# Hybrid attention trunk on one core: the low part of k laid on all 128 rows, and weight staging in the q/k/v slots

## The chip, the core and the metric

The kernel runs on one core of a Trainium2 chip. The metric is the device time of one execution in microseconds, the median over several runs. A profiled execution gives in addition the span of the program and the time of every instruction on TensorE (PE; its weight loads are listed apart, as PEld), VectorE (DVE), ScalarE (ACT), GpSimd (POOL) and on SyncE's queue (SP), which issues the DMAs.

## The reference, cut to what matters

Two residual layers over 1024 positions of width 1024, each followed by a gated MLP with a short convolution. The first layer splits one projection between differential attention (4 heads, causal) and a pooling mixer, joins both and projects out. The second is sliding-window attention with 16 query heads in 4 groups of 4, window 128. What matters for the change are the scores of both attentions, a product of q and k over 64 channels of a head:

```
# first layer: h heads, m = 2 maps, d = 64 channels
s = jnp.einsum('bqhmd,bkhmd->bhmqk', qi, kf) * scale + bias
# second layer: 128 queries against their own and the previous 128 keys
s = jnp.einsum('bqhgd,bkhd->bhgqk', qi, kb) * scale + bias
```

and the projections by the weights `ab_w_in`, `ab_w_out`, `c_w_in`, `c_w_out`, `w_up` and `w_down`, which the kernel loads in slabs of 128x1024.

## The kernel before

Every fp32 operand is split into a high part, rounded to the fast matmul type, and a low part, the remainder. A product is three matmuls, high*high, high*low and low*high (`mm3`, L96 to L102). A weight slab is loaded by `load_split` (L127): a DMA on SP's queue brings it as fp32 into a staging tile, ACT writes the high part (L109), POOL the low part (L110), both into tiles of the pool tag `ws`. The staging tile is free once POOL has read it.

All large tiles have 4 KB on each of 128 partitions and come from rings by tag, of a fixed number of slots (`BUFS`, L76): `x` 8, `xg` 16, `g` 9, `t` 5, `wr` 2, `ws` 8. `wr` is the staging of raw weights, and of the four slabs of the pooling mixer's result that come back from DRAM (L661). `g` holds the tiles of q, k and v in the attentions, the split result of the pooling mixer and, in the MLP, the gated activations. A tile may be written when the tile that had its slot before is read for the last time; within a tag the slots are handed out in the order in which the program asks for them.

The stages follow each other: the pooling mixer's inputs and the mixer itself (`a_pool`, `a_mix`), the projections of the first layer, its attention (`a_attend`, four heads of eight query blocks j), its output projection, the MLP, the projections of the second layer, its attention (`c_attend`, four groups of eight blocks), its output projection, and the second MLP. While a head or a group runs, other dense work is woven between its blocks by `weave`: the projections of the next heads and groups (L344 is the matmul of `in_tokens` in them), and, in the last two heads and groups, the first part of the output projection (`project_out`, L101 into the banks `psd`). The order of the instructions on each engine is then set by the framework's scheduler from its own estimate of times, so a change in the tiles moves instructions everywhere. Each engine runs its instructions in the order so set.

In a head, `stack_q` builds two tiles of q: in tile m one half of the rows holds the high part of map m's 64 channels, the other half the low part. `stack_k` builds for each m a tile of 128 rows with the high part of k in both halves (L400, L401 on ACT), and one more tile `lo`, in which the rows of half m hold the low part of map m (L402, DVE). A score is two matmuls into one bank (`scores`, L406): L410 contracts 128 rows, (q high; q low) by (k high; k high), and L411 adds q high by k low over the 64 rows of the half m alone. The score then goes to DVE (L481 or L741, which add the table and take the running minimum), to ACT (exp, L485 or L745), through transposes (L505, L763), a second split (L109 on ACT, L110 on DVE, into `hf` tiles), and into the product by v (L516, L101 into `psq`).

Of the kernel before, what the change touches and what calls it, by code (L numbers as in the profile page):

```python
# [13 lines left out]
F32 = mybir.dt.float32  # L14
F32R = mybir.dt.float32r
I32 = mybir.dt.int32
AF = mybir.ActivationFunctionType
# [46 lines left out]
class Trunk:  # L64
# [8 lines left out]
        self.pd = mk("spill", 1, space=bass.MemoryType.DRAM)  # L73
        self.n = 0

    BUFS = {"x": 8, "xg": 16, "g": 9, "t": 5, "wr": 2, "ws": 8}  # L76

    def big(self, tag, dt=F32, shape=(P, 1024)):
        self.n += 1
# [46 lines left out]

    def load_split(self, src, tag="ws", shape=(P, 1024), eng=None):  # L127
        nc = self.nc
        raw = self.big("wr", F32, shape)
        nc.sync.dma_start(raw[:], src)  # L130
        hi = self.big(tag, F32R, shape)
        lo = self.big(tag, F32R, shape)
        with self.urgent():
            self.split(raw[:], hi[:], lo[:], eng or nc.gpsimd)
        return hi, lo
# [252 lines left out]
                    out=dst[other, sl], in0=pt[rows, :], scalar=gain[rows, :], in1=dst[rows, sl].bitcast(F32),  # L388
                    op0=ALU.mult, op1=ALU.subtract)

    def stack_k(self, get, gain, his, lo):
        nc = self.nc
        for h in range(2):
            pt = self.bank()
            for b in range(4):
                nc.tensor.transpose(pt[:, b * P:(b + 1) * P], get(4 * h + b), self.idn[:])
            sl = slice(h * HALF, (h + 1) * HALF)
            for m, hi in enumerate(his):
                rows, other = slice(m * 64, (m + 1) * 64), slice((1 - m) * 64, (2 - m) * 64)
                nc.scalar.activation(hi[rows, sl], pt[rows, :], AF.Copy, scale=gain[rows, :])  # L400
                nc.scalar.activation(hi[other, sl], pt[rows, :], AF.Copy, scale=gain[rows, :])  # L401
                nc.vector.scalar_tensor_tensor(  # L402
                    out=lo[rows, sl], in0=pt[rows, :], scalar=gain[rows, :], in1=hi[rows, sl].bitcast(F32),
                    op0=ALU.mult, op1=ALU.subtract)

    def scores(self, out, m, q, k, qs, ks):  # L406
        nc = self.nc
        his, lo = k
        rows = slice(m * 64, (m + 1) * 64)
        nc.tensor.matmul(out, q[:, qs], his[m][:, ks], start=True, stop=False)  # L410
        nc.tensor.matmul(out, q[rows, qs], lo[rows, ks], start=False, stop=True)  # L411

    def project_qk(self, w, norm, raws, bank="d"):
        xg, r, _ = norm
# [34 lines left out]
    def a_attend(self, h, raws, vs, o, before, tails):  # L449
        nc, I = self.nc, self.I  # L450
        tab = self.big("t")
        nc.sync.dma_start(tab[:], I["tab_a"][h])
        q = [self.big("g", F32R) for _ in range(2)]
        k = ([self.big("g", F32R) for _ in range(2)], self.big("g", F32R))
        get = lambda o: (lambda b: raws[b // 4][:, (b % 4) * 256 + o:(b % 4) * 256 + o + P])
        self.stack_q(get(0), self.gq[:, 0:1], q)
        self.stack_k(get(P), self.par[:, PAR_AK:PAR_AK + 1], *k)
# [153 lines left out]
    def layer_a(self, w, norm, bd, after):  # L611
# [38 lines left out]
        def project_out():  # L650
            for i in range(2):
                am[i] = self.split_mix(mixes[i], "xg")
            x.extend(self.load_x(I["xT"]))
            for ks in ((4, 5, 6, 7), (0, 1)):
                ws, ms = [], []
                for k in ks:
                    ws.append(self.load_split(I["a_out"][k]))
                    if k < 4:
                        ms.append(am[k])
                        continue  # L660
                    raw = self.big("wr")  # L661
                    nc.sync.dma_start(raw[:], bd[(k - 4) * P:(k - 3) * P, :])
                    ms.append(self.split_mix(raw, "xg"))
                yield from self.contract(ws, [self.halves(m) for m in ms], x, banks="d")
# [30 lines left out]
    def c_project_kv(self, w, norm, bank="s"):  # L695
# [11 lines left out]
                out=vl[:, sl], in0=po[:, P:], scalar=r[:, b:b + 1], in1=vh[:, sl].bitcast(F32),  # L707
                op0=ALU.mult, op1=ALU.subtract)
        self.head_norm(ms, r, 2, [raw], NB)
        k = ([self.big("g", F32R) for _ in range(2)], self.big("g", F32R))  # L710
        self.stack_k(lambda b: raw[:, b * P:(b + 1) * P], self.par[:, PAR_CK:PAR_CK + 1], *k)
        return k, (vh, vl)

# [271 lines left out]
```

## Time and profile before

| | |
|---|---|
| time of the runs | 2301.35 us median of 3 (2295.84 to 2303.99) |
| span of the profiled execution | 2294.5 us, 6.9 us less than the median |
| PE busy | 2243.8 us, 98% of the span |
| DVE busy | 1466.6 us, 64% |
| ACT busy | 807.0 us, 35% |
| POOL busy | 598.6 us, 26% |
| DMA engines | 17.2% of their time on the main queue |
| attention of the first layer | first score at 132 us, last transpose of its output at 441 us |
| second layer's attention | first score at 1250 us, last score at 1533 us |

A number such as "128x512" is partitions by columns. The time of one matmul in the trace runs from its start to its modelled end and overlaps the next one, since matmuls are pipelined; what a matmul costs in a row of them is the distance between starts. The granted clock of TensorE (PEclk) is given as a share of 2.4 GHz, so 0.50 is 1.2 GHz.

### The profile page before, as it was taken

How to read it: one execution, taken by the hardware profiler on the slowest of the kernel's cores; microseconds unless marked ns; L12 is line 12 of the kernel's file. 1: busy time of each engine (PE TensorE's matmuls, PEld its weight loads, DVE VectorE, ACT ScalarE, POOL GpSimd, SP SyncE). 2: the span in 40 equal slices, each digit the busy share in tenths (PEclk: the TensorE clock that was granted, in tenths of full speed). 3: DMA queues.
4: the chain of work that ended last, by engine and by line, in shares of the span. 5: the costliest groups of instructions: out<-in, count | busy, mean ns of one | idle time of the engine just before them, and what ended most of it. 6: DMA issues, size and time to landing. Idle time of an engine off the chain costs nothing.

```text
span 2294.5 us, 28081 instructions
## 1 busy us (share of the span) xinstructions
PE 2243.8 (98%) x11176; PEld 1863.3 (81%) x11176; DVE 1466.6 (64%) x2421; ACT 807.0 (35%) x1432; POOL 598.6 (26%) x314
## 2 busy tenths in 40 slices
PE   6999999999999999999999998999999999999999
PEld 4988867878888888888889876778888888888887
DVE  7666787775556555555675767667755555556655
ACT  4365555442222222222245566445222222222220
POOL 5210031342221222222252324245122222222120
PEclk9999999999999999999999998999999999999999
DMA  4210122011111111111131101111111111111111
GB/s 157 76 45 28 55 84 65 19 56 47 55 47 37 55 55 47 46 55 47 57 111 38 40 17 56 38 59 44 37 55 55 46 48 54 46 46 38 55 55 74
DMA packets 40019, 123.07 MB, mean 54 GB/s; under 512 B 4688, under 2 KB 5200, under 8 KB 39888
## 3 DMA queue, kind: packets, MB, share of 16 engines
q1 hardware_dynamic: 39888, 121.28, 17.2%
q8 instruction: 88, 1.44, 0.3%
q14 instruction: 43, 0.35, 0.1%
HBM read 110.78 MB, written 10.49 MB: 53 GB/s over the span
## 4 chain that ended last, share of the span: by engine, by line
PE 90%; DVE 7%; ACT 1%; issue 1%; DMA 0%; POOL 0%; SPq 0%; DVEq 0%; POOLq 0%; ACTq 0%
PE pss L101 41%; PE psd L101 16%; PE psq L101 14%; PE psd L344 7%; PE pss L344 3%; PE pss L411 3%; PE pss L410 2%; DVE xg L205 2%; PE psq L516 1%; PE psq L763 1%; DVE x L254 1%; PE psq L505 1%; PE psq L382 0%; DVE nt L147 0%; DVE ny L153 0%
## 5 line engine op out<-in xcount | busy, mean ns | idle before, releaser
L101 PE MATMUL pss<-xg,ws 128*128 128x512 f32 x4296 | 998.1, 390 | 16.7 <-ACT ws L109 8.7
L101 PEld LDWEIGHTS pss<-xg,ws 128*128 128x128 f32 x4296 | 805.8, 188 | 189.3 <-DVE xg L205 10.4
L110 POOL TENSOR_TENSOR ws<-wr,ws 128x1024 fp32r<-128x1024 f32 x172 | 417.6, 2434 | 1279.1 <-ACT ws L109 1271.5
L109 ACT ACTIVATE ws<-wr 128x1024 fp32r<-128x1024 f32 x174 | 181.9, 1057 | 642.1 <-PE pss L101 368.3
L101 PE MATMUL psq<-g,ws 128*128 128x512 f32 x1296 | 320.2, 389 | 0.0
L276 DVE TENSOR_TENSOR t<-pss,rbc 128x512 f32<-128x512 f32 x172 | 118.2, 688 | 277.4 <-PE pss L101 277.0
L101 PEld LDWEIGHTS psq<-g,ws 128*128 128x128 f32 x1296 | 242.4, 188 | 49.9
L279 DVE SCALAR_TENSOR_TENSOR t<-t,conv,t 128x1023 f32<-128x1023 f32 x88 | 202.1, 2296 | 87.3 <-ACT t L278 87.3
L254 DVE TENSOR_TENSOR x<-psd,x 128x512 f32<-128x512 f32 x224 | 153.8, 687 | 142.8 <-PE psd L101 141.3
L101 PE MATMUL psd<-g,ws 128*128 128x512 f32 x960 | 240.3, 389 | 0.0
L101 PEld LDWEIGHTS psd<-g,ws 128*128 128x128 f32 x960 | 180.2, 188 | 37.4
L344 PE MATMUL psd<-ws,xg 128*128 128x256 f32 x1344 | 191.6, 292 | 0.5 <-DVE hms L353 0.5
L344 PEld LDWEIGHTS psd<-ws,xg 128*128 128x128 f32 x1344 | 170.1, 192 | 12.6 <-issue 4.3
L254 DVE TENSOR_TENSOR x<-psq,x 128x512 f32<-128x512 f32 x224 | 150.9, 683 | 38.1 <-PE psq L101 37.8
L101 PE MATMUL psd<-xg,ws 128*128 128x512 f32 x624 | 167.3, 409 | 0.0
L109 ACT ACTIVATE g<-t 128x1024 fp32r<-128x1024 f32 x49 | 52.0, 1061 | 257.7 <-DVE t L300 249.0
L101 PEld LDWEIGHTS psd<-xg,ws 128*128 128x128 f32 x624 | 113.6, 191 | 27.3 <-issue 1.9
L281 DVE SCALAR_TENSOR_TENSOR t<-t,conv,t 128x1022 f32<-128x1022 f32 x88 | 112.6, 1279 | 2.3
L278 ACT ACTIVATE t<-t,conv 128x1024 f32<-128x1024 f32 x88 | 108.7, 1235 | 7.4 <-DVE t L276 4.4
L296 ACT ACTIVATE t<-t 128x1024 f32<-128x1024 f32 x44 | 46.6, 1060 | 153.7 <-DVE t L281 153.7
L344 PE MATMUL pss<-ws,xg 128*128 128x256 f32 x768 | 96.3, 283 | 0.2 <-DVE hms L353 0.2
L344 PEld LDWEIGHTS pss<-ws,xg 128*128 128x128 f32 x768 | 94.9, 191 | 2.0 <-DVE hms L353 0.4
(162 smaller groups left out, 2195.6 us busy)
## 6 DMA issues: line engine op xcount, KB each, us to landing
wr<-in_dram SPq DMA_DIRECT2D x174, 512.0 KB, 3.6
x<-in_dram SPq DMA_DIRECT2D x32, 256.0 KB, 3.8
t<-in_dram SPq DMA_DIRECT2D x8, 512.0 KB, 3.6
xd<-x SPq DMA_DIRECT2D x16, 256.0 KB, 2.0
x<-xd SPq DMA_DIRECT2D x16, 256.0 KB, 3.0
out_dram<-x SPq DMA_DIRECT2D x16, 256.0 KB, 2.0
bd<-t SPq DMA_DIRECT2D x4, 512.0 KB, 3.0
wr<-bd SPq DMA_DIRECT2D x4, 512.0 KB, 3.4
```

Source lines behind the costliest of these rows:

```text
L101: self.nc.tensor.matmul(out, a, b, start=(k == 0), stop=(k == n - 1))
L109: nc.scalar.activation(hi, raw, AF.Copy)
L110: (eng or nc.vector).tensor_tensor(out=lo, in0=raw, in1=hi.bitcast(F32), op=ALU.subtract)
L205: nc.vector.scalar_tensor_tensor(out=lo[:, sl], in0=x, scalar=g, in1=hi[:, sl].bitcast(F32), op0=ALU.mult, op1=ALU.subtract)
L254: nc.vector.tensor_tensor(out=xs, in0=po[:], in1=xs, op=ALU.add)
L276: nc.vector.tensor_tensor(out=hr[:, sl], in0=ps[h][:], in1=rbc[:, sl], op=ALU.mult)
L278: nc.scalar.activation(c[:], hr[:], AF.Identity, bias=cw(3), scale=cw(2))
L279: nc.vector.scalar_tensor_tensor(out=c[:, 1:], in0=hr[:, :S - 1], scalar=cw(1), in1=c[:, 1:], op0=ALU.mult, op1=ALU.add)
L281: nc.vector.scalar_tensor_tensor(out=c[:, 2:], in0=hr[:, :S - 2], scalar=cw(0), in1=c[:, 2:], op0=ALU.mult, op1=ALU.add)
L296: nc.scalar.activation(th[:], cg[:], AF.Tanh, scale=0.5)
L344: self.nc.tensor.matmul(out, a, m[:, d % 4, :], start=(n == 0), stop=(n == 23))
L411: nc.tensor.matmul(out, q[rows, qs], lo[rows, ks], start=False, stop=True)
```

## The change

`g` gets 11 slots in place of 9, and the tag `wr` goes: `load_split` and `project_out` take their staging tile from `g`. `stack_k` makes two low tiles, one for each m. DVE writes the low part into half m of tile m as before, and a new instruction on ACT copies it into the other half (64x512, 2 halves of columns by 2 maps, in each of the four heads and once for the second layer: 20 instructions). The second matmul of a score then takes all 128 rows: (q high; q low) by (k low; k low), which also adds the product of the two low parts. Lines from L404 on have numbers one higher after the change: the score matmuls L410 and L411 are L411 and L412 there.

```diff
@@ -73,7 +73,7 @@
         self.pd = mk("spill", 1, space=bass.MemoryType.DRAM)
         self.n = 0
 
-    BUFS = {"x": 8, "xg": 16, "g": 9, "t": 5, "wr": 2, "ws": 8}
+    BUFS = {"x": 8, "xg": 16, "g": 11, "t": 5, "ws": 8}
 
     def big(self, tag, dt=F32, shape=(P, 1024)):
         self.n += 1
@@ -126,7 +126,7 @@
 
     def load_split(self, src, tag="ws", shape=(P, 1024), eng=None):
         nc = self.nc
-        raw = self.big("wr", F32, shape)
+        raw = self.big("g", F32, shape)
         nc.sync.dma_start(raw[:], src)
         hi = self.big(tag, F32R, shape)
         lo = self.big(tag, F32R, shape)
@@ -388,7 +388,7 @@
                     out=dst[other, sl], in0=pt[rows, :], scalar=gain[rows, :], in1=dst[rows, sl].bitcast(F32),
                     op0=ALU.mult, op1=ALU.subtract)
 
-    def stack_k(self, get, gain, his, lo):
+    def stack_k(self, get, gain, his, los):
         nc = self.nc
         for h in range(2):
             pt = self.bank()
@@ -399,16 +399,17 @@
                 rows, other = slice(m * 64, (m + 1) * 64), slice((1 - m) * 64, (2 - m) * 64)
                 nc.scalar.activation(hi[rows, sl], pt[rows, :], AF.Copy, scale=gain[rows, :])
                 nc.scalar.activation(hi[other, sl], pt[rows, :], AF.Copy, scale=gain[rows, :])
+                lo = los[m]
                 nc.vector.scalar_tensor_tensor(
                     out=lo[rows, sl], in0=pt[rows, :], scalar=gain[rows, :], in1=hi[rows, sl].bitcast(F32),
                     op0=ALU.mult, op1=ALU.subtract)
+                nc.scalar.activation(lo[other, sl], lo[rows, sl].bitcast(F32), AF.Copy)
 
     def scores(self, out, m, q, k, qs, ks):
         nc = self.nc
-        his, lo = k
-        rows = slice(m * 64, (m + 1) * 64)
+        his, los = k
         nc.tensor.matmul(out, q[:, qs], his[m][:, ks], start=True, stop=False)
-        nc.tensor.matmul(out, q[rows, qs], lo[rows, ks], start=False, stop=True)
+        nc.tensor.matmul(out, q[:, qs], los[m][:, ks], start=False, stop=True)
 
     def project_qk(self, w, norm, raws, bank="d"):
         xg, r, _ = norm
@@ -451,7 +452,7 @@
         tab = self.big("t")
         nc.sync.dma_start(tab[:], I["tab_a"][h])
         q = [self.big("g", F32R) for _ in range(2)]
-        k = ([self.big("g", F32R) for _ in range(2)], self.big("g", F32R))
+        k = tuple([self.big("g", F32R) for _ in range(2)] for _ in range(2))
         get = lambda o: (lambda b: raws[b // 4][:, (b % 4) * 256 + o:(b % 4) * 256 + o + P])
         self.stack_q(get(0), self.gq[:, 0:1], q)
         self.stack_k(get(P), self.par[:, PAR_AK:PAR_AK + 1], *k)
@@ -658,7 +659,7 @@
                     if k < 4:
                         ms.append(am[k])
                         continue
-                    raw = self.big("wr")
+                    raw = self.big("g")
                     nc.sync.dma_start(raw[:], bd[(k - 4) * P:(k - 3) * P, :])
                     ms.append(self.split_mix(raw, "xg"))
                 yield from self.contract(ws, [self.halves(m) for m in ms], x, banks="d")
@@ -707,7 +708,7 @@
                 out=vl[:, sl], in0=po[:, P:], scalar=r[:, b:b + 1], in1=vh[:, sl].bitcast(F32),
                 op0=ALU.mult, op1=ALU.subtract)
         self.head_norm(ms, r, 2, [raw], NB)
-        k = ([self.big("g", F32R) for _ in range(2)], self.big("g", F32R))
+        k = tuple([self.big("g", F32R) for _ in range(2)] for _ in range(2))
         self.stack_k(lambda b: raw[:, b * P:(b + 1) * P], self.par[:, PAR_CK:PAR_CK + 1], *k)
         return k, (vh, vl)
 
```

In an attention of the first layer the tag `g` holds 4 tiles of v, 2 of q and 3 of k before (9 of 9 slots), and 4, 2 and 4 after (10 of 11), where the raw weights for the dense work pass through the slots that are left. In the second layer it is 2 of v, 4 of q and 3 or 4 of k.

How the order moves is shown at three places. The first is SP's queue at the start, from the load of the second slab of the pooling mixer's input weights on (a row is the line, the target and the source; the numbers after the names count the tiles; `hf_289` is the pooling mixer's own weight, `hf_637` the lambda vectors, and the rows of L130 are weight slabs: 429 is the last of the mixer's input weights). Before:

```order
L130 DMA wr_348<-in_dram 128x1024
L265 DMA conv_4983<-in_dram 128x176
L130 DMA wr_429<-in_dram 128x1024
L130 DMA wr_513<-in_dram 128x1024
L130 DMA wr_519<-in_dram 128x1024
L130 DMA wr_646<-in_dram 128x1024
L615 DMA hf_289<-in_dram 128x512
L177 DMA hf_637<-in_dram 128x256
L130 DMA wr_652<-in_dram 128x1024
```

After:

```order
L130 DMA g_348<-in_dram 128x1024
L265 DMA conv_5003<-in_dram 128x176
L616 DMA hf_289<-in_dram 128x512
L177 DMA hf_637<-in_dram 128x256
L130 DMA g_429<-in_dram 128x1024
L585 DMA bd<-t_417 128x1024
L130 DMA g_513<-in_dram 128x1024
L130 DMA g_519<-in_dram 128x1024
L585 DMA bd<-t_501 128x1024
```

The load of the slab 429 stands behind the two small loads, and those of 513 and 519 behind the mixer's first store (L585). On PE the mixer's first matmuls (`psq` from `hf`) stand ahead of the 48 matmuls that take slab 429, where before they stood behind those 48 and behind 15 of L344.

The second place is PE's order at the start of the second layer's attention (L396 and L382 are the transposes of `stack_k` and `stack_q`, L344 dense projection work for the next group). Before, the end of 137 rows of L344 that stand between the projection of k and v and the first score:

```order
L344 MATMUL psd_10669<-ws_10286,xg_9358 128x256
L344 MATMUL psd_10669<-ws_10286,xg_9359 128x256
L344 MATMUL psd_10669<-ws_10287,xg_9359 128x256
L344 MATMUL psd_10669<-ws_10286,xg_9360 128x256
L382 MATMUL psq_10249<-idn,x_9676 128x128 x4
L410 MATMUL pss_10352<-g_10199,g_10236 128x256
L411 MATMUL pss_10352<-g_10201,g_10236 128x256
L382 MATMUL psq_10258<-idn,x_9675 128x128 x4
```

After:

```order
L344 MATMUL pss_10164<-ws_9692,xg_9379 128x256
L344 MATMUL pss_10164<-ws_9691,xg_9380 128x256
L396 MATMUL psq_10223<-idn,x_9950 128x128 x4
L396 MATMUL psq_10236<-idn,x_9950 128x128 x4
L382 MATMUL psq_10265<-idn,x_9695 128x128 x4
L382 MATMUL psq_10274<-idn,x_9696 128x128 x4
L382 MATMUL psq_10283<-idn,x_9695 128x128 x4
L411 MATMUL pss_10377<-g_10219,g_10261 128x256
L412 MATMUL pss_10377<-g_10221,g_10261 128x256
L382 MATMUL psq_10292<-idn,x_9696 128x128 x4
```

None of those 137 matmuls stands ahead of the first score any more; the first two L344 for the next group come after the ninth score.

The third place is PE's order early in the third group of that attention (g = 2; `psd` from `xg` and `ws` is the output projection's first part, `psq` from `hf` the product by v). Before:

```order
L763 MATMUL psq_11918<-idn,t_11890 128x128 x4
L101 MATMUL psd_12717<-xg_12583,ws_12620 128x512
L101 MATMUL psd_12717<-xg_12582,ws_12621 128x512
L101 MATMUL psd_12717<-xg_12582,ws_12626 128x512
L101 MATMUL psd_12717<-xg_12583,ws_12626 128x512
L101 MATMUL psd_12717<-xg_12582,ws_12627 128x512
L101 MATMUL psd_12642<-xg_12586,ws_12632 128x512
L410 MATMUL pss_12295<-g_10199,xg_11761 128x256
L411 MATMUL pss_12295<-g_10201,xg_11761 128x256
L410 MATMUL pss_12234<-g_10199,xg_11762 128x256
L411 MATMUL pss_12234<-g_10201,xg_11762 128x256
L410 MATMUL pss_12235<-g_10200,xg_11764 128x256
```

After:

```order
L411 MATMUL pss_12065<-g_10219,xg_11787 128x256
L412 MATMUL pss_12065<-g_10221,xg_11787 128x256
L764 MATMUL psq_11854<-idn,t_11826 128x128 x4
L411 MATMUL pss_12144<-g_10219,xg_11787 128x256
L412 MATMUL pss_12144<-g_10221,xg_11787 128x256
L411 MATMUL pss_12145<-g_10220,xg_11788 128x256
L412 MATMUL pss_12145<-g_10222,xg_11788 128x256
L764 MATMUL psq_11859<-idn,t_11826 128x128 x4
L411 MATMUL pss_12066<-g_10220,xg_11789 128x256
L412 MATMUL pss_12066<-g_10222,xg_11789 128x256
L411 MATMUL pss_12259<-g_10219,xg_11786 128x256
L412 MATMUL pss_12259<-g_10221,xg_11786 128x256
```

The dense matmuls of 512 columns have gone from between the scores: of 67 that stood between the first and the last score of this group none is left there, and in the last group 72 of 140. Together with those between the groups, 198 of them now stand behind the last score.

## Rows read from the trace of the kernel before

**Rows 1.** The page: busy time and share by engine; the chain that ended last.

```profile
PE 2243.8 (98%) x11176; PEld 1863.3 (81%) x11176; DVE 1466.6 (64%) x2421; ACT 807.0 (35%) x1432; POOL 598.6 (26%) x314
...
PE 90%; DVE 7%; ACT 1%; issue 1%; DMA 0%; POOL 0%; SPq 0%; DVEq 0%; POOLq 0%; ACTq 0%
```

**Rows 2.** Timeline, first layer: start us, us, engine, line, operation [idle before <-releaser].

```profile
247.28 0.39 PE L410 MATMUL pss<-g,g 128*128 128x512 f32 x1
...
247.61 0.49 PE L411 MATMUL pss<-g,g 64*128 64x512 f32 x1
...
248.03 0.53 PEld L344 LDWEIGHTS psd<-ws,xg 128*128 128x128 f32 x4 [0.24 <-issue]
248.03 0.74 PE L344 MATMUL psd<-ws,xg 128*128 128x256 f32 x4
```

**Rows 3.** Timeline, second layer: two scores in a row.

```profile
1405.28 0.39 PE L410 MATMUL pss<-g,xg 128*128 128x256 f32 x1
...
1405.59 0.38 PE L411 MATMUL pss<-g,xg 64*128 64x256 f32 x1
1405.90 0.42 PEld L101 LDWEIGHTS psq<-hf,g 128*128 128x128 f32 x3
```

**Rows 4.** PE's timeline just ahead of the second layer's first score.

```profile
1243.51 6.59 PE L344 MATMUL psd<-ws,xg 128*128 128x256 f32 x53
1249.94 0.60 PE L382 MATMUL psq<-idn,x 128*128 128x128 f32 x4
```

**Rows 5.** Timeline at the start, PE and DVE.

```profile
55.90 8.20 PE L101 MATMUL pss<-xg,ws 128*128 128x512 f32 x35
...
60.05 0.16 DVE L153 SCALAR_TENSOR_TENSOR r<-nt,ny 128x4 f32<-128x4 f32 x1
...
63.94 1.05 PE L233 MATMUL psd<-idn,r 128*128 128x128 f32 x8
...
71.53 1.23 DVE L110 TENSOR_TENSOR g<-t,g 128x1024 fp32r<-128x1024 f32 x1 [1.13 <-ACT g L109]
...
74.59 0.63 PE L101 MATMUL psq<-g,hf 128*128 128x512 f32 x2
```

**Rows 6.** Windows by stage: us, PE busy (instructions), PEld, DVE, ACT, POOL, PEclk, DMA.

```profile
132.00:284.00 152.00, 149.26 (x1054) 130.46 (x1053) 111.27 (x330) 85.79 (x211) 14.53 (x10) 1.00 0.12 37
284.00:360.00 76.00, 74.03 (x349) 55.56 (x348) 61.74 (x161) 39.36 (x93) 21.81 (x15) 0.93 0.25 76
360.00:441.00 81.00, 80.14 (x377) 60.68 (x376) 65.41 (x166) 39.63 (x86) 22.55 (x12) 1.00 0.18 54
1231.00:1250.00 19.00, 18.52 (x156) 18.31 (x155) 10.90 (x27) 10.83 (x23) 4.87 (x3) 1.00 0.19 56
1250.00:1328.00 78.00, 74.12 (x524) 65.35 (x522) 58.78 (x168) 47.20 (x133) 23.98 (x14) 1.00 0.12 35
1328.00:1390.00 62.00, 56.30 (x338) 46.12 (x338) 43.64 (x140) 38.94 (x117) 19.28 (x13) 0.94 0.09 26
1390.00:1466.00 76.00, 74.71 (x362) 57.89 (x362) 49.80 (x134) 42.84 (x113) 26.18 (x14) 0.91 0.14 47
1466.00:1533.00 67.00, 67.00 (x337) 51.86 (x337) 44.93 (x122) 35.09 (x94) 24.76 (x12) 1.00 0.16 50
```

**Rows 7.** Windows of three stretches with little dense work, same columns.

```profile
292.00:302.00 10.00, 9.82 (x24) 6.16 (x24) 8.57 (x26) 6.55 (x17) 5.04 (x4) 0.51 0.43 133
302.00:316.00 14.00, 13.09 (x60) 8.46 (x59) 13.71 (x32) 8.72 (x23) 8.96 (x5) 0.99 0.47 150
1390.00:1405.00 15.00, 13.71 (x37) 9.04 (x37) 10.28 (x23) 11.70 (x26) 7.14 (x4) 0.54 0.30 105
```

**Rows 8.** The page: the low part of a slab on POOL; the slab's DMA.

```profile
L110 POOL TENSOR_TENSOR ws<-wr,ws 128x1024 fp32r<-128x1024 f32 x172 | 417.6, 2434 | 1279.1 <-ACT ws L109 1271.5
...
wr<-in_dram SPq DMA_DIRECT2D x174, 512.0 KB, 3.6
```

**Rows 9.** Groups by form: the nearest ACT form to the added copy.

```profile
L400 ACT ACTIVATE g<-psq,par 64x512 fp32r<-64x512 f32 x20 | 13.6, 682 | 8.1 <-DVE g L402 5.3 <-PE psq L396 2.4
```

## The prediction

> **What bounds the kernel now.** First the page: TensorE (PE) is busy 98% of the span, and the chain of waits that ended last is 90% PE, 7% VectorE (DVE) [rows 1]. Time can only be won where PE gets less to do, as long as nothing else takes its place. Then the windows by stage, to see how far the next engine is behind in the two attentions, the only stages whose matmuls change: DVE works 111 of 152 us in heads 0 and 1, 62 of 76 in head 2, 50 of 76 and 45 of 67 in groups 2 and 3 of the second layer [rows 6]. Then the timeline around single scores, for the price of the half-array matmul. Last the order of the changed kernel, since the scheduler has moved work between the stages.
>
> **The saving on PE.** A full matmul that stands among its like costs PE 0.121 us at 256 columns (53 in 6.43 us, from the first start to the next row's) and 0.230 us at 512 (35 in 8.04 us) [rows 4, 5]. A score does not run at that rate: L410 to L411 takes 0.33 us and L411 to the next matmul 0.42 us at 512 columns, 0.31 and 0.31 us at 256 [rows 2, 3]. The weight load behind an L411 does not run ahead of it but sits idle, 0.24 us, until the next matmul may start [rows 2]: PE empties when it goes from 128 rows to 64 and again on the way back. The excess of one L411 is so (0.33 + 0.42) - 2 x 0.230 = 0.29 us, or 0.62 - 2 x 0.121 = 0.38 us. There are 96 in the first layer and 128 in the second: 224 x 0.29 to 0.38 = 65 to 85 us; I take 0.335 us and 75 us, 32 in the first and 43 in the second layer. After the change both matmuls of a score are of the full form, with nothing to switch.
>
> The trace of before has 53 full matmuls with 128x128 loads in a row at 0.121 us each [rows 4], so a full load hides behind a full matmul. The Trainium skill, "TensorE: Matmul & The Clock Gate", Part 3, "What overlaps and what doesn't", says against this change that a weight load overlaps with matmuls in flight only when its row group differs. By that each L412 would wait out a load, and by the row's distances some 0.15 us of every 0.335 would remain, a saving of about 41 us; the trace disagrees with it, and the sum goes on by 75.
>
> **What is added.** 20 copies on ScalarE (ACT), 64x512. The nearest row is L400, the same shape out of PSUM: 0.682 us [rows 9], 13.6 us in all, 2.7 us per head. ACT is busy 35% [rows 1], and in the heads the k of the next head is built under the dense work of the one before; there they cost nothing. At the second layer's start that cover goes (below). DVE, POOL and DMA get nothing new.
>
> **What is moved.** The raw weights now queue for the slots of q, k and v, and one staged slab holds its slot for the DMA (3.6 us), ACT's and POOL's part (2.43 us) [rows 8], some 7 us with the high part between. Dense work whose slabs come later stands later on PE, and PE runs in order. So I go stage by stage.
>
> *Start.* The mixer's first matmuls now stand ahead of the 48 matmuls of slab 429. Before, they ran at 74.59, when their operand, ready at 71.53 + 1.23 = 72.76, was long there [rows 5]. The chain to it: r is ready at 60.21, PE's L233 took it up at 63.94, the operand follows 8.8 us later. After, L233 stands ahead of those 48, so it can start at 60.3 and the operand is there at 69.1. PE's work ahead of it is done earlier: what ran until 63.94 less those rows of slab 429 that stood there, about 58.8, then a wait of 1.5 us for r, 1.05 us of L233 and 12 matmuls of 0.23 us, about 64.0. PE waits 1.5 + 5.1 = 6.6 us that it did not wait before, and DVE's lambda step, which stands further ahead and waits for a DMA, can add a little: I take 7 us lost, 0 to 9.
>
> *Heads 0 and 1* (152 us, PE 149.3, DVE 111.3 [rows 6]): 48 scores with 0.335 us less are 16 us; the order has 351 + 369 L344 in place of 356 + 340, 24 x 0.121 = 3 us more. 2.7 us of idle stay and DVE is far off: 11 us won.
>
> *Head 2* (76 us, PE 74.0, DVE 61.7): 8 us from the scores; and the order has 84 dense matmuls of 512 columns for 144, and none for 24 L344: 13.8 + 2.9 = 16.7 us moved to head 3 and behind. The rest of PE is 49 us, so DVE sets the pace. In the stretch after 302 us, with little dense work, DVE was busy 13.71 of 14 us [rows 7], a share of 0.98: 61.7 / 0.98 = 63 us, 13 won. *Head 3 to 441 us* (81, PE 80.1): less 8, plus 16.7 moved in, less the 3 that went to heads 0 and 1: 5 to 6 us lost. First layer: 11 + 13 - 6 = 18; since dense work in head 2 stands in one lump behind the scores I take 15, 8 to 20.
>
> *Second layer's start* (19 us, PE 18.5 [rows 6]): 137 L344, 16.5 us, have left it, their slab waits its turn in a single slot; what remains is the chain through transposes, ACT and DVE, bare. ACT worked 10.8 us there and gets 2.7 more, so it cannot be under 13.5; it was hidden within 19 and can be 21.7. I take 19: nothing won.
>
> *Groups 0 and 1* (78 and 62 us): they lose 10.7 us of PE each and get 55 and 89 L344 more, 6.6 and 10.7 us. In group 0 these stand behind the 25th score: by the order's rows at the rates above PE has 15 us ahead of that, DVE 24 (DVE sets it), and PE 52 behind: 76 us. Group 1 likewise 59. Won: 2 + 3 = 5.
>
> *Groups 2 and 3* (76 and 67 us to the last score, 143 together): 130 dense matmuls leave group 2 and 68 of 140 group 3; the 198 stand behind the last score, where DVE and ACT have little left that could hide them: 198 x 0.23 = 45 us more there. PE keeps 74.7 - 10.7 - 29.9 = 34 us in group 2, 67.0 - 10.7 - 15.6 = 41 in group 3, less than DVE's 49.8 and 44.9 [rows 6]. So DVE and the chain through it set the length, X = 94.7 / s, where s is DVE's busy share. Rows for s are 0.98 (302 to 316 us), 0.86 (292 to 302, granted clock 0.51, that is 1.2 GHz) and 0.69 (1390 to 1405, clock 0.54) [rows 7]. The last two are stretches with PE busy 98% and 91% because of its clock and of L411's emptying; after the change PE has less there. I take s = 0.92, X = 103 us: 40 won against 45 lost. Second layer: 0 + 5 + 40 - 45 = 0, between -10 (s = 0.86) and +7 (s = 0.98).
>
> The clock is a part of this: where PE idled it fell to 0.51 in the stretch after 292 us [rows 7], and bare groups give it more such places; the range of s holds that. The MLPs and projections keep their order of matmuls, and their slabs come from a ring of 11 in place of 2; PE there waits for nothing of the staging now, and I count 0.
>
> **The sum.** 15 + 0 - 7 = 8 us: a span of 2286.5 us. The profiled execution's span lay 6.9 us under the median, so 2293.4, say 2293 us, 0.36% faster, right at the bound of 0.3% (6.9 us), which is about what a measurement of this kernel can tell from no change. Of the 75 us, some 65 are given back: 45 behind the last score, 7 at the start, the rest to DVE's pace. With the ends of the terms (first layer 8 to 20, second -10 to +7, start 0 to -9) its own range is 2278 to 2310.
>
> **The rivals.**
>
> *More of the saving is kept.* If the bare groups run at DVE's pure work as the order leaves it, 88 us for groups 2 and 3 (some of DVE's work, the splits of v and q for the last blocks, moves behind with the rest), the start does not stall and the first layer keeps its full 32 us: 32 + 5 + 55 - 45 = 47 us, 2254; with all 75 kept 2226. For it: PE is 90% of the chain [rows 1], and 0.98 was seen [rows 7]. Against: PE's idle time is already small, and every term must go well at once.
>
> *Slower: the bare groups wait.* The place is groups 2 and 3, whose scores stand without dense work. If a block's chain (score, DVE, exp on ACT, DVE, POOL, transpose, split, product) isn't overlapped enough by five tiles `t` and three banks `pss`, DVE idles as it did in 1390 to 1405, s = 0.69: X = 137 us, 6 won against 45 lost, 2293 + 34 = 2327 us. It decides from s = 0.85 on, where the whole comes to zero (X = 111), and by s = 0.80 the kernel is slower by 0.3%. For it: these very rows, in the very group. Against: PE was the busy engine there.
>
> *The change does not do what it says:* a full L412 that shares its weights' place with L411 still empties PE. Then nothing is saved, the moves remain, and 45 us behind the last score are met by less: about 2310 to 2340. Rows 4 speak against it.
>
> **How the numbers follow.** The forecast gets 0.53, of it 0.28 under 2294.4, 0.19 within 0.3%, 0.06 slower. More kept: 0.17, all faster. The bare groups wait: 0.25, of it 0.20 slower, 0.05 within. Nothing saved: 0.05, slower. So faster 0.45, same 0.24, slower 0.31. The time is the forecast's, 2293 us. The range leaves out one in ten on either side: 2262 cuts the upper half of the saving, 2322 the worst of the bare groups.
>
> **What would show it.** Score to score in the changed trace at 0.12 us (256) and 0.23 us (512) per matmul, with no idle ahead of the loads: the saving. PE idle of 5 to 8 us near 60 to 70 us, ended by DVE's split of the mixer: the start. Head 2 at 63 us, groups 2 and 3 together at about 103 with DVE at 0.9, and some 45 us more between the last score and the MLP: the moves. The forecast is wrong if the bare groups keep their 143 us, or if the dense work behind the last score hides what else ends there, so that its 45 us are met by less than 45.

## The result, and the profile after

The changed kernel takes 2306.73 us (median of 7 runs, 2305.63 to 2308.19), the kernel before 2299.49 us in the runs beside it: a ratio of 1.003, with an interval of 1.0019 to 1.0041. It is slower by 0.3%, about 7 us. The forecast was 2293 us, 0.36% faster; the time lies in the range, but the sign is the other one. The profiled execution has a span of 2304.9 us, 10.4 us more than before.

The page of the changed kernel, engines and chain (compare [rows 1]):

```profile
PE 2199.5 (95%) x11176; PEld 1869.3 (81%) x11176; DVE 1414.3 (61%) x2421; ACT 815.6 (35%) x1452; POOL 614.7 (27%) x314
...
PE 82%; DVE 11%; ACT 3%; issue 2%; POOL 1%; DMA 1%; SPq 0%; DVEq 0%; POOLq 0%; ACTq 0%
```

PE has 44 us less to do and still the end comes later: its share of the chain falls from 90 to 82%, DVE's rises from 7 to 11% and ACT's from 1 to 3%, and POOL and DMA get 1% each. First the scores, on PE's timeline in head 1 (start us, us; compare [rows 2]):

```profile
238.98 0.39 PE L411 MATMUL pss<-g,g 128*128 128x512 f32 x1
239.21 0.39 PE L412 MATMUL pss<-g,g 128*128 128x512 f32 x1
239.44 1.83 PE L344 MATMUL psd<-ws,xg 128*128 128x256 f32 x14
```

Both distances are 0.23 us where they were 0.33 and 0.42. The emptying of PE is gone, as the change says. This can be added up over the whole trace. Each matmul is taken at the median distance from its kind to the next matmul (0.11, 0.12, 0.18 or 0.23 us for 128 to 512 columns), which makes 2129 us in both kernels. What the distances have beyond that is called the emptying where a 64-row matmul stands on either side and no wait ends there: 77 us before (the expectations have 76.6) and 0 after. The remainder is waits and slow clock: 75 us before and 163 after. So 77 us were saved and 88 us lost. The windows by stage say where (us, PE busy, PEld, DVE, ACT, POOL, PEclk, DMA; compare [rows 6]):

```profile
141.00:275.00 134.00, 133.73 (x1076) 131.25 (x1074) 106.40 (x325) 89.87 (x221) 16.84 (x12) 1.00 0.12 37
275.00:351.00 76.00, 55.93 (x266) 43.18 (x265) 66.23 (x168) 46.48 (x101) 24.36 (x16) 0.84 0.31 102
351.00:436.00 85.00, 81.28 (x419) 67.74 (x418) 64.33 (x163) 38.37 (x84) 19.95 (x10) 1.00 0.22 71
1229.00:1244.00 15.00, 4.80 (x23) 3.85 (x22) 7.90 (x23) 8.81 (x16) 0.10 (x1) 0.79 0.00 0
1244.00:1324.00 80.00, 75.41 (x578) 73.72 (x577) 55.21 (x154) 49.80 (x140) 25.11 (x15) 0.89 0.11 34
1324.00:1382.00 58.00, 54.08 (x425) 52.63 (x423) 43.48 (x141) 39.01 (x119) 19.23 (x12) 0.94 0.06 19
1382.00:1435.00 53.00, 39.76 (x228) 34.80 (x228) 47.31 (x138) 39.05 (x111) 26.17 (x14) 0.81 0.15 51
1435.00:1490.00 55.00, 46.35 (x275) 37.85 (x275) 38.83 (x111) 36.37 (x99) 22.23 (x11) 1.00 0.30 96
1490.00:1590.00 100.00, 91.67 (x428) 75.62 (x428) 60.43 (x92) 34.03 (x57) 48.24 (x26) 0.96 0.18 58
```

Heads 0 and 1 fall from 152 to 134 us with PE full. Head 2 takes 76 us as before, but PE works only 56 of them. Groups 2 and 3 fall from 143 to 109 us, and the stretch behind the last score, 54 us before, takes 99. What keeps the output projection out of groups 2 and 3 is on SP's queue. In the kernel before, the first four slabs of the output projection, counted along the queue (100 loads of slabs stand ahead of them in both kernels), are the last two of the row at 1233.72 (issued at 1262.0 and 1264.4 us) and the two at 1312.87, all in group 0; the next two follow in group 1, ahead of the loads of x:

```profile
1233.72 30.99 SPq L130 DMA_DIRECT2D wr<-in_dram  x4
...
1312.87 5.01 SPq L130 DMA_DIRECT2D wr<-in_dram  x2
...
1371.21 0.33 SPq L130 DMA_DIRECT2D wr<-in_dram  x1
...
1378.65 0.38 SPq L130 DMA_DIRECT2D wr<-in_dram  x1
1396.97 30.08 SPq L595 DMA_DIRECT2D x<-xd  x8
```

In the changed one the first four come in group 3, behind most of the loads of x:

```profile
1389.41 22.54 SPq L596 DMA_DIRECT2D x<-xd  x8
...
1433.74 4.44 SPq L596 DMA_DIRECT2D x<-xd  x6
1438.23 17.76 SPq L130 DMA_DIRECT2D g<-in_dram  x3
...
1467.41 24.70 SPq L130 DMA_DIRECT2D g<-in_dram  x6
```

The first of these slabs comes 176 us later than before. With it come the matmuls: the first of the output projection's first part runs at 1396.6 us before and at 1444.3 after.

### The profile page after: what moved, and what is told of

Same layout as the page of the kernel before. It is cut to its first block, busy times and chain, and to the rows that moved or that the text cites. A ratio compares the mean times of both kernels' runs of the same rounds, so it can differ in the third digit from the quotient of the medians.

```text
span 2304.9 us, 28148 instructions
## 1 busy us (share of the span) xinstructions
PE 2199.5 (95%) x11176; PEld 1869.3 (81%) x11176; DVE 1414.3 (61%) x2421; ACT 815.6 (35%) x1452; POOL 614.7 (27%) x314
## 4 chain that ended last, share of the span: by engine, by line
PE 82%; DVE 11%; ACT 3%; issue 2%; POOL 1%; DMA 1%; SPq 0%; DVEq 0%; POOLq 0%; ACTq 0%
PE pss L101 41%; PE psq L101 14%; PE psd L101 13%; PE psd L344 6%; PE pss L344 4%; DVE xg L205 2%; PE psq L517 1%; DVE t L742 1%; DVE x L254 1%; PE pss L411 1%; PE pss L412 1%; DVE t L482 1%; PE psq L764 1%; DVE hf L110 1%; DMA g<-in_dram 1%
## 5 line engine op out<-in xcount | busy, mean ns | idle before, releaser
L101 PE MATMUL pss<-xg,ws 128*128 128x512 f32 x4296 | 1000.9, 393 | 18.7 <-ACT ws L109 12.4
L110 POOL TENSOR_TENSOR ws<-g,ws 128x1024 fp32r<-128x1024 f32 x172 | 432.4, 2525 | 1260.3 <-ACT ws L109 956.7
L276 DVE TENSOR_TENSOR t<-pss,rbc 128x512 f32<-128x512 f32 x172 | 118.3, 689 | 335.9 <-PE pss L101 332.9
L109 ACT ACTIVATE ws<-g 128x1024 fp32r<-128x1024 f32 x174 | 178.2, 1048 | 237.9 <-issue 209.4
L254 DVE TENSOR_TENSOR x<-psd,x 128x512 f32<-128x512 f32 x224 | 154.0, 689 | 164.4 <-PE psd L101 164.3
L344 PE MATMUL psd<-ws,xg 128*128 128x256 f32 x1344 | 185.4, 288 | 0.3 <-DVE hms L353 0.3
L254 DVE TENSOR_TENSOR x<-psq,x 128x512 f32<-128x512 f32 x224 | 151.3, 686 | 53.9 <-PE psq L101 53.8
L344 PEld LDWEIGHTS psd<-ws,xg 128*128 128x128 f32 x1344 | 173.8, 195 | 2.3 <-DVE hms L353 0.8
L279 DVE SCALAR_TENSOR_TENSOR t<-t,conv,t 128x1023 f32<-128x1023 f32 x88 | 113.7, 1292 | 86.7 <-ACT t L278 86.7
L101 PE MATMUL psd<-xg,ws 128*128 128x512 f32 x624 | 159.4, 398 | 7.9 <-ACT xg L109 2.3
L281 DVE SCALAR_TENSOR_TENSOR t<-t,conv,t 128x1022 f32<-128x1022 f32 x88 | 154.9, 1761 | 2.3
L109 ACT ACTIVATE g<-t 128x1024 fp32r<-128x1024 f32 x49 | 52.0, 1061 | 212.4 <-DVE t L300 202.4
L217 POOL TENSOR_TENSOR hf<-hf,hf 128x512 f32<-128x512 f32 x56 | 83.4, 1489 | 55.0 <-ACT hf L211 39.3
L344 PE MATMUL pss<-ws,xg 128*128 128x256 f32 x768 | 96.8, 286 | 0.0
L344 PEld LDWEIGHTS pss<-ws,xg 128*128 128x128 f32 x768 | 95.7, 194 | 1.2
```

The source lines that it names most:

```text
L101: self.nc.tensor.matmul(out, a, b, start=(k == 0), stop=(k == n - 1))
L109: nc.scalar.activation(hi, raw, AF.Copy)
L110: (eng or nc.vector).tensor_tensor(out=lo, in0=raw, in1=hi.bitcast(F32), op=ALU.subtract)
L217: eng.tensor_tensor(out=acc[:], in0=acc[:], in1=sq[:], op=ALU.add)
L254: nc.vector.tensor_tensor(out=xs, in0=po[:], in1=xs, op=ALU.add)
L276: nc.vector.tensor_tensor(out=hr[:, sl], in0=ps[h][:], in1=rbc[:, sl], op=ALU.mult)
```

## The experiments

Nine kernels, each timed against the kernel before on the same chip. Ratios are to that kernel, with their 95% intervals. In the tables of stages below, times run from the first score of a head or group to the next in the profiled execution. Differences to the changed kernel are between medians; by the ratios they come out up to 2 us larger or smaller.

**The 128-row score alone.** The kernel before with one line changed: both low parts are in one tile already, rows 0 to 63 for m = 0 and the rest for m = 1, so all its rows can be taken.

```diff
-        nc.tensor.matmul(out, q[rows, qs], lo[rows, ks], start=False, stop=True)
+        nc.tensor.matmul(out, q[:, qs], lo[:, ks], start=False, stop=True)
```

> The kernel before with one line changed: L411 becomes q[:, qs] x lo[:, ks], all 128 rows of the one shared low tile. Rows of the other map's half then meet the low part of q and add (q low)*(low part of the other map), a term of the size of the low*low product that the split drops anyway. No fourth k tile, no copy, wr keeps its two slots. Theory (the emptying of PE at L411 costs 76.6 us in the trace of before, and what gave it back in the changed kernel is the staging through g): nearly the whole is kept, 2235 us (2225 to 2250). Rival (DVE and the chain pace the attentions, so PE time won there is idle again, whatever the staging does): waits take its place here too, 2280 us or more.

Measured: 2240.88 us, ratio 0.974 (0.9725 to 0.9756), 60 us less than before. The theory holds: without the moves of the staging most of the saving is kept. Page and two windows (groups 2 and 3):

```profile
PE 2170.2 (97%) x11176; PEld 1852.2 (83%) x11176; DVE 1465.4 (65%) x2421; ACT 803.4 (36%) x1432; POOL 598.3 (27%) x314
```

```profile
1357.00:1422.00 65.00, 62.39 (x375) 55.22 (x374) 46.06 (x132) 40.09 (x110) 26.31 (x15) 0.96 0.15 50
1422.00:1478.00 56.00, 51.96 (x318) 45.54 (x317) 42.04 (x119) 34.49 (x95) 24.61 (x12) 1.00 0.22 67
```

Here PE keeps its dense work between the scores, and the stretch behind the last one is 56 us. A part of the rival is true: waits and slow clock rise from 75 to 100 us, in heads 2 and 3 above all, where PE waits 9.0 us for DVE's running minimum in place of 1.8. So 25 of the 77 us are given back, in good part to DVE's pace, even here. This kernel beats the one before and the changed one.

**The merged staging alone.** The kernel before with `g` 11, no `wr`, both raw tiles from `g`, nothing else.

```diff
-    BUFS = {"x": 8, "xg": 16, "g": 9, "t": 5, "wr": 2, "ws": 8}
+    BUFS = {"x": 8, "xg": 16, "g": 11, "t": 5, "ws": 8}
...
-        raw = self.big("wr", F32, shape)
+        raw = self.big("g", F32, shape)
...
-                    raw = self.big("wr")
+                    raw = self.big("g")
```

> The kernel before with the staging alone merged: g 11 slots, no wr, scores still over 64 rows with one low tile, no copies. Theory (the merged ring moves the loads behind q, k and v, and so dense work away from the places it covered): 30 to 45 us slower than before, about 2335 us, with PE waits at the start, ahead of group 0 and in group 2. Rival (merging is harmless while nine tiles leave two slots; it is the fourth k tile and the copies that cost): within 7 us of before.

Measured: 2344.55 us, ratio 1.0188 (1.0167 to 1.021), 43 us slower. The theory holds, and the rival falls: nine tiles leave two slots free, and the merging costs all the same. The first score comes at 138.6 us (132.1 before), the start of the second layer's attention lacks 136 of its 143 L344, and group 2 has none of its dense matmuls, though group 3 gets more. Its windows for groups 0, 2 and 3:

```profile
1254.00:1347.00 93.00, 92.62 (x615) 82.05 (x613) 56.04 (x157) 51.90 (x143) 23.84 (x14) 0.90 0.10 29
...
1410.00:1468.00 58.00, 52.28 (x228) 38.73 (x226) 48.51 (x137) 39.34 (x109) 26.15 (x14) 0.74 0.14 46
1468.00:1559.00 91.00, 88.45 (x405) 68.81 (x405) 48.30 (x122) 37.09 (x99) 27.38 (x13) 0.92 0.19 59
```

**The changed kernel with its staging apart.** `g` 10, `wr` 1, as much memory as changed and before; two low tiles, copies and 128-row scores stay.

```diff
-    BUFS = {"x": 8, "xg": 16, "g": 11, "t": 5, "ws": 8}
+    BUFS = {"x": 8, "xg": 16, "g": 10, "t": 5, "wr": 1, "ws": 8}
...
-        raw = self.big("g", F32, shape)
+        raw = self.big("wr", F32, shape)
...
-                    raw = self.big("g")
+                    raw = self.big("wr")
```

> The changed kernel with the staging taken apart again: g 10 slots, wr 1 slot; two low tiles, the 20 copies and the 128-row scores stay. Theory (the shared ring costs, not the copies): the second layer gets its dense work back between the scores (order: 142 and 122 matmuls of 512 columns in groups 2 and 3), head 2 stays short of it (72 of 144), so about 2255 us (2240 to 2270). Rival (one staging slot and the copies cost as much as the shared ring): 2290 us or more.

Measured: 2256.17 us, ratio 0.9804 (0.979 to 0.9819). The theory holds within some 1 us: one slot of its own for the staging does better than a ring of 11 shared with q, k and v. Against the one-line kernel the fourth tile, the copies and the lost staging slot cost 15 us.

**The changed kernel with the 64-row matmul put back.**

```diff
-        nc.tensor.matmul(out, q[:, qs], los[m][:, ks], start=False, stop=True)
+        rows = slice(m * 64, (m + 1) * 64)
+        nc.tensor.matmul(out, q[rows, qs], los[m][rows, ks], start=False, stop=True)
```

> The changed kernel with the 64-row second matmul put back (rows of half m of los[m]); tiles, copies and merged staging as changed. Theory: in the stretches where PE now waits (head 2, start of the second layer, groups 2 and 3) part of the emptying hides in the waits, in the others it counts: 45 us slower than the changed kernel, about 2350 us (2335 to 2365). If all 76.6 us count: 2383. Rival (the emptying is hidden wherever DVE sets the pace, and the saving was worth little from the start): 2315 us or less.

Measured: 2375.69 us, ratio 1.0323 (1.0304 to 1.0341), 69 us over the changed kernel. That is above the expected 2335 to 2365 and near the end where all counts. By the count used above, the emptying is 96 us in this trace, more than the 77 of before, since more of it falls at the slower clock, and PE's waits with slow clock elsewhere fall by 26, from 163 to 136. So most of it shows, even where DVE sets the pace: in the changed kernel the 128-row score is worth nearly the full 77 us, and it is the rest of the change that took this away.

**Merged staging with the one low tile and 128 rows.** The first two edits together.

> Staging merged as in the change, 128-row scores by the one shared low tile: no fourth k tile and no copies, so two slots are left for the staging in the first layer's heads. With the kernel before, the 128-row score alone (2240.9) and the merging alone (2344.6) it closes the square. If saving and loss only add up: 2344.6 - 60.4 = 2284 us (2276 to 2292). Rival (the stretches left bare by the merging are paced by DVE and can't use the saving): 2305 us or more. Against the changed kernel (2306.7) the difference is then the price of the fourth k tile with its copies under merged staging, some 20 to 30 us.

Measured: 2294.69 us, ratio 0.9982 (0.9971 to 0.9993), between the two expectations. The table has what stands now, in ratios to the kernel before:

| | staging apart | staging in g |
|---|---|---|
| 64 rows, one low tile | 1 | 1.0188 |
| 128 rows, one low tile | 0.974 | 0.9982 |
| 64 rows, two low tiles with copies | | 1.0323 |
| 128 rows, two low tiles with copies | 0.9804 (one slot) | 1.003 |

The 128-row score is worth 2.6% with the staging apart and 2.1 to 2.9% with it merged; the merging costs 1.9 to 2.4%, the second low tile 0.5 to 1.35%. By the ratios the merging costs 56 us with 128 rows, some 12 more than with 64. From apart to merged, waits and slow clock grow from 100 to 150 us with 128 rows; with 64 rows they grow from 75 to 109, and the emptying from 77 to 90. So between the two kernels with merged staging and one low tile the 128-row score wins 50 us, little more than half of the 90 that the emptying has there: what it leaves free is in part waited away.

**The copies on POOL.**

```diff
-                nc.scalar.activation(lo[other, sl], lo[rows, sl].bitcast(F32), AF.Copy)
+                nc.gpsimd.tensor_copy(lo[other, sl], lo[rows, sl].bitcast(F32))
```

> The changed kernel with the 20 copies put on POOL instead of ACT. Theory (the copies on ACT stand in the chain to head 2's first scores: PE waits 6.1 us for them there): 2300 us (2296 to 2304). Rival (the chain waits for DVE and the next ACT step anyway, the copies only happen to come last): no change, 2304 us or more, or slower if POOL's copy takes longer than ACT's 0.63 us.

Measured: 2309.88 us, ratio 1.0048 (1.0033 to 1.0063), no gain. The theory falls: PE's waits for the copy in head 2 (two, 5.6 us together) are gone, but waits for DVE take their place: PE's waits in head 2 add up to 19.9 us with the copies on ACT and 20.0 on POOL, and the head takes 78 us for 76. That the copy came last in the chain did not make it the cause.

**The second group's slab asked for earlier.**

```diff
         wk = self.in_weights(I["c_kv"])
+        w1 = self.in_weights(I["c_q"][1])
...
-                yield from self.project_qk(self.in_weights(I["c_q"][g]), norm, qs[g])
+                yield from self.project_qk(w1 if g == 1 else self.in_weights(I["c_q"][g]), norm, qs[g])
```

> The changed kernel with one thing moved: the slabs of the second group's projection are asked for ahead of the k, v and q tiles of the second layer (same slots, same loads). Theory (the place of a request in the program sets its slot, and so when its dense work runs): the order has 144 more L344 ahead of the first score again, PE's 13.8 us of waiting there go and groups 0 and 1 get some of it back as their own: 2295 us (2288 to 2300). Rival (that work is only missing later, in groups 0 and 1, whose scores it covers now): 2303 us or more.

Measured: 2307.49 us, ratio 1.0032 (1.0015 to 1.0048), no change. Windows of the stretch ahead of the first score, and of groups 0 and 1:

```profile
1231.00:1250.00 19.00, 18.66 (x157) 18.42 (x156) 10.20 (x29) 12.76 (x27) 0.10 (x1) 1.00 0.00 1
1250.00:1320.00 70.00, 61.90 (x471) 60.24 (x469) 53.18 (x160) 44.23 (x129) 20.10 (x12) 0.93 0.08 24
1320.00:1381.00 61.00, 52.90 (x383) 50.45 (x384) 45.20 (x128) 38.20 (x116) 19.28 (x13) 0.86 0.06 18
```

The slot's place in the program does set where the work stands: PE works 18.7 of 19 us ahead of the first score again. But the three stretches together take 150.2 us where the changed kernel takes 152.2. The work that came back is missing in groups 0 and 1, where PE's waits are now 16.2 us in place of 8.4. The rival holds: within this stage it hardly matters where the cover stands.

**The output projection's slabs asked for earlier.**

```diff
             for g in range(1, NG):
-                yield from self.project_qk(self.in_weights(I["c_q"][g]), norm, qs[g])
+                w = self.in_weights(I["c_q"][g])
+                if g == NG - 1:
+                    wo.extend(self.load_split(I["c_out"][t]) for t in range(2))
+                yield from self.project_qk(w, norm, qs[g])
...
-                ws = [self.load_split(I["c_out"][2 * g + t]) for g in gs for t in range(2)]
+                ws = [wo.pop(0) if wo else self.load_split(I["c_out"][2 * g + t]) for g in gs for t in range(2)]
```

> The changed kernel with the first two slabs of the second layer's output projection asked for earlier, with the last group's projection slabs and so ahead of the last group's q tiles; nothing else. In the order 12 and 186 dense matmuls of 512 columns then stand in groups 2 and 3 (0 and 72 in the changed kernel). Theory (what costs is the dense work behind the last score, 0.23 us a matmul): 126 x 0.23 = 29 us come back less what groups 2 and 3 get longer by, 2282 us (2276 to 2290). Rival (as with the first slab: the work only trades places with DVE's waits, group 3 gets longer by as much): 2300 us or more.

Measured: 2295.17 us, ratio 0.9975 (0.9964 to 0.9986), 11.5 us less than the changed kernel. Windows of group 2, group 3 and the stretch behind the last score:

```profile
1383.00:1434.00 51.00, 38.32 (x242) 32.71 (x241) 46.63 (x139) 39.84 (x111) 26.29 (x15) 0.93 0.17 53
1434.00:1508.00 74.00, 69.83 (x388) 59.87 (x388) 43.41 (x123) 33.90 (x96) 18.85 (x10) 0.98 0.17 55
1508.00:1580.00 72.00, 68.09 (x326) 56.55 (x326) 54.06 (x80) 34.77 (x61) 43.73 (x25) 0.98 0.23 76
```

Between theory and rival. Behind the last score 26.7 us come back (99.4 to 72.7 us), near the 29 that the count of matmuls says, but group 3 grows by 17.9 us (55.9 to 73.8), since the 114 matmuls that went there are 26 us and only 8 of them lie in its waits.

**The first layer's output slabs asked for earlier.**

```diff
-                    ws.append(self.load_split(I["a_out"][k]))
+                    ws.append(wo.pop(0) if wo else self.load_split(I["a_out"][k]))
...
             if h == 2:
+                wo.extend(self.load_split(I["a_out"][k]) for k in (4, 5))
                 vs = self.split_v(vb)
```

> The changed kernel with the first two slabs of the first layer's output projection asked for ahead of head 2's v, q and k tiles; nothing else. The order puts 24 dense matmuls more into head 2 (108 for 84). Theory (head 2's 36 us of waits and slow clock come from the dense work it lacks): 24 x 0.23 = 5.5 us, up to 10 with the clock, 2299 us (2296 to 2303). Rival (head 2 is paced by DVE, 66 of 76 us, so more dense work there changes nothing): 2305 us or more.

Measured: 2301.36 us, ratio 0.9998 (0.9986 to 1.0011), 5.4 us less than the changed kernel. The time lies where the theory put it, with its smaller number: 24 matmuls of 0.23 us.

```profile
274.00:350.00 76.00, 59.04 (x290) 48.12 (x289) 62.24 (x168) 43.09 (x97) 20.02 (x14) 0.87 0.26 82
```

Head 2 takes its 76 us as in the changed kernel, with 3 us more of PE's busy time in it, as the rival said of the head alone; head 3 is the shorter for it.

## Why the prediction was wrong, step by step

The stretches of the attentions run from score to score, as above; an MLP starts with DVE's first L276.

| stretch of the profiled execution | forecast, us | measured, us |
|---|---|---|
| start to the first score | +7 | +8.5 |
| heads 0 and 1 | -11 | -17.9 |
| head 2 | -13 | -0.2 |
| head 3 to the first MLP | +6 | +1.6 |
| first MLP | 0 | +5.2 |
| second layer's projections | 0 | +0.6 |
| ahead of its first score | 0 | -3.8 |
| groups 0 and 1 | -5 | -2.4 |
| groups 2 and 3 | -40 | -33.6 |
| last score to the second MLP | +45 | +45.7 |
| second MLP | 0 | +6.8 |

The prediction lowered the heads' terms by 3 us, to a sum of -15 for the first layer; the forecast's sum is -8, the measured one +10.4.

**The saving** was right: 75 us forecast, 77 by the trace of before, nothing left after. The rule of the Trainium skill that was weighed there ("TensorE: Matmul & The Clock Gate", Part 3, on weight loads and row groups) does not hold here: full loads hide behind full score matmuls, 0.23 us from start to start.

**The start** was right in its size, 8.5 us for 7, but in part by luck. DVE and PE there, after (compare [rows 5]):

```profile
41.90 1.16 PE L233 MATMUL psd<-idn,r 128*128 128x128 f32 x8 [1.56 <-DVE r L153]
...
46.11 0.29 DVE L180 TENSOR_TENSOR hf<-hf 128x128 f32<-128x128 f32 x1 [2.20 <-DMA hf<-in_dram]
...
47.37 11.20 PE L101 MATMUL pss<-xg,ws 128*128 128x512 f32 x36 [3.18 <-DVE x L557]
58.41 1.05 PE L233 MATMUL psd<-idn,r 128*128 128x128 f32 x8
...
65.42 0.73 PE L101 MATMUL psq<-g,hf 128*128 128x512 f32 x2 [3.20 <-ACT g L109]
...
69.58 2.07 PE L101 MATMUL pss<-xg,ws 128*128 128x512 f32 x4 [0.96 <-ACT ws L109]
```

The mixer's matmuls wait 3.2 us for their operand, less than the 5.1 worked out, and L233 at 58.41 does not wait for r, which was put at 1.5. The lambda step stands on DVE ahead of L557, for which PE waits 3.2 us; that was put at "a little". But the L233 at 41.90, with its wait of 1.6 us, has the longer wait in the kernel before:

```profile
45.01 2.08 PE L233 MATMUL psd<-idn,r 128*128 128x128 f32 x8 [5.83 <-DVE r L153]
```

So all of PE's waits up to the first score grow by 1.2 us only, from 10.9 to 12.1. Most of the rest is the clock, which the sum did not have here: the 36 matmuls from 47.37 on take 11.0 us, where 0.227 us each would be 8.2, and the granted clock from 60 to 85 us is 0.86 where it was 1.00 from 56 to 83 us before.

**The first layer** came out near its sum for other reasons than given. Heads 0 and 1 won 7 us more: their scores' 16 us came whole, and 5 us of waits and slow clock went too. Head 2 was put at 63 us by DVE's share of 0.98 of 61.7 us, and took 76: DVE was busy 66 of 76, a share of 0.87, with 20 us of waits on PE and a granted clock of 0.84. That these misses, and the 4 us of head 3, nearly cancel is luck. The row taken for s stood in the middle of a head with its chain filled; head 2 after the change starts bare (PE waits 3.6 us there for the first low tile).

**Groups 2 and 3** have X = 109 us with DVE busy 86 of them, s = 0.79. The forecast took 0.92 of a larger DVE time and got 103, 6 us too few. That this is the rival's s (0.80) with a time far from the rival's is because DVE's work there fell as well, from 95 to 86 us: the adds of the output projection to x (L254) moved behind the last score with their matmuls, 19.9 us of them in groups 2 and 3 before and 4.1 after, while DVE's other work there grew somewhat.

**The step that failed** was to count nothing where a moved step meets what stands behind it, twice; next to it, the share s was put too high in both bare stretches (0.98 for 0.87, 0.92 for 0.79). Behind the last score the moved matmuls cost 45 us as worked out, but a part of them runs past the start of the second MLP (6.1 us of matmul work more stands behind that mark, nearly all of the +6.8), and the MLP's norm, which had dense work beside it, now stands bare:

```profile
1571.10 9.23 PE L101 MATMUL pss<-xg,ws 128*128 128x512 f32 x40
1587.20 2.07 PE L233 MATMUL psd<-idn,r 128*128 128x128 f32 x8 [6.88 <-DVE r L153]
```

Before, the same step stood there with no wait ahead of it:

```profile
1581.21 1.05 PE L233 MATMUL psd<-idn,r 128*128 128x128 f32 x8
```

So that term is 52 us, not 45. And in the first MLP the slabs' high parts, once their tiles come from `g`, stand on ACT behind the MLP's own steps; "PE there waits for nothing of the staging" was wrong:

```profile
497.22 1.24 ACT L278 ACTIVATE t<-t,conv 128x1024 f32<-128x1024 f32 x1 [1.42 <-DVE t L276]
498.37 1.04 ACT L109 ACTIVATE ws<-g 128x1024 fp32r<-128x1024 f32 x1
...
499.46 0.74 PE L101 MATMUL pss<-xg,ws 128*128 128x512 f32 x2 [2.41 <-ACT ws L109]
```

This one wait and the slower clock behind it are most of the 4.5 us more than before that are lost in that MLP. The same wait, 2.4 us by ACT's L109, is in the first MLP of all eight kernels with merged staging, and in none of the three that have it apart. But one staging slot has a price there too: the kernel with `wr` 1 waits 5.8 us in its first MLP, for DVE's L276. The stretch behind the last score with the second MLP is 7 us over the forecast, the first MLP 5, the start 1.5, groups 2 and 3 6: some 20 us, of which the other stretches give 2 back, and that is the way from -8 to +10.

**The rivals.** That more of the saving is kept needed what the one-line kernel has, the staging left alone; it gives 2241. That nothing is saved is out. Of the third, the mechanism is there, DVE idle in bare groups, with its place and its share; its price was smaller, and the sign came in the main from the terms put at nothing.

What stays open is why the scheduler places the slabs so late with two slots free, as in the kernel with merging alone. That the request's place in the program moves them was shown for three pairs of slabs; that it explains all of them was not tried.

## What to carry to other kernels

A matmul over half the rows between matmuls over all of them costs more than one over all rows (0.31 us against 0.12 at 256 columns here), so fill the rows with something harmless; look for what is in the tile already before paying for a copy. Staging buffers that feed the busiest engine are better left a ring of their own: of the same memory, one slot apart did better here (0.9804) than eleven shared with long-lived tiles (1.003), since the place of the loads moved with the sharing. When an edit moves work of the bound engine behind a stage, price not only the moved work but also what used to run beside what now stands behind it.

## What the runs showed of the hardware that was not expected

PE's clock takes part in most of the bare stretches: the granted clock was 0.81 in group 2 and 0.84 in head 2 of the changed kernel, a mean over pieces at 2.4 and at 1.2 GHz in stages where PE waited for DVE again and again, against 0.91 and 0.93 before; in group 3, where 72 dense matmuls are left, it was 1.00. Over the whole kernel, time lost on PE beside waits and emptying rises from 30 to 55 us, and the mean granted clock falls from 0.991 to 0.976. How much of the emptying for 64-row matmuls shows depends on what stands around it: taking it out won 60 of 77 us with the staging apart and 50 of 90 with it merged, and putting it back into the changed kernel cost 69 of 96.
